# Half of an up-projection in Strassen units, merged rows added by DMA, embedding pairs moved

## The chip, the cores and the metric

The kernel runs on one NeuronCore of a Trainium2 chip. Its engines work side by side, each with a queue of its own: TensorE (PE, matmuls; its weight loads are shown as PEld), VectorE (DVE), ScalarE (ACT), GpSimd (POOL) and SyncE (SP, which here only issues DMAs). An engine takes its instructions in the order of its queue, and one that waits holds back all behind it. The metric is device time in microseconds; lower is better. Everything is float32 in DRAM; on PE each number is split into a high and a low part (type fp32r), and a product is three matmuls: high·high, high·low, low·high.

## The reference

One decoder layer, 512 tokens, width 2048 (all weights are inputs):

```python
proj = rmsnorm(x, attn_norm_g) @ w_in          # u, v_sgu, q, k, v_att, g_a, g_b
y_a = chunked_spatial_gating(gelu(u), rmsnorm(gelu(v_sgu)))     # 512 x 1024
y_b = stick_breaking_attention(rmsnorm(q), rmsnorm(k), v_att)   # 512 x 1024
merged = sigmoid(g_a) * (y_a @ w_up_a) + sigmoid(g_b) * (y_b @ w_up_b)
x = x + merged @ w_o
hid = rmsnorm(x, ffn_norm_g) @ w_ffn_in
x = x + (silu(gate) * up) @ w_ffn_out          # gate, up: halves of hid
x = x + sigmoid(rmsnorm(x, ple_norm_g) @ w_ple_gate) * (p @ w_ple)
```

## The kernel before

**Units.** Activations lie transposed (features by tokens) and are cut into blocks of 256 features by 512 tokens. One block against 256 columns of weights is a *unit*, and all units that sum to the same 256 outputs are a *pair* (`pair()`, class `Pair`). A unit is plain ("P": 12 matmuls of 512 columns) or Strassen ("S": seven products of a 2 x 2 scheme, 21 matmuls of 256 columns, or 7 of 512 and 7 of 256 where the pair asks for the `doubled` form with a bank of its own for each product). Tables such as `HALF` say until which pair of a stage each unit stays plain: the operand of a Strassen unit needs three more sums of the block, and plain pairs at a stage's start give time to make them.

**Operands.** A `Form` makes one operand: it loads the block (`fetch`), splits it into high and low (`plain_first`: ACT the high, DVE the low), later loads it a second time (`fetch_second`) and makes the sums. `tick()` is called once or twice per unit pair: it fetches one block, runs one step of one form or, if none is due, fetches one second half, and runs what `after(n, ...)` put n ticks ahead. `Weights` does the same for weights: two SP loads, a POOL DMA that adds in SBUF (L361), a split on ACT (L357) and DVE (L354), and two sums (L373). Four landing places and three split places are shared by all weights.

**Stages.** (1) w_in: q, k, v and gate pairs in four rounds, with attention of each round run beside the next pairs in steps of a tick (`attention`: stages a, m, b, c, d per block of 128 keys, then `finish`, which multiplies by v); then the gating half. Gate pairs are spilled to DRAM. (2) The up-projection: for each of 8 column blocks j a pair of w_up_b, then one of w_up_a, four plain units each. A gate block is loaded, scaled by the norm's row and put through the sigmoid; DVE multiplies it with the two banks (L1350), adds the b part to the a part (L1354), and SP stores the merged block (L1332, DRAM tensor mix). (3) w_o: eight pairs of eight units on mix, with x added (L792) and stored (DRAM tensor x). The last pairs of the embedding product p @ w_ple follow: two before the last addition, three after it. (4) w_ffn_in, 44 pairs; (5) w_ffn_out in three passes, added to x in DRAM by POOL's DMA (L1430); (6) the last gate.

**Order.** The order is written out by `tick` and `after`; within it a scheduler sets each engine's queue. The last pair of a matmul stage frees its operands unit by unit, and the next stage's take their places, so a stage's border is where operands come just in time.

## Time and profile before

| What | us |
|---|---|
| Median of 3 runs | 2669.71 |
| Lowest and highest | 2667.64, 2671.62 |
| Profiled execution | 2668.2 |
| Its span, first to last instruction | 2666.5 |
| PE busy in it | 2640.4 |
| Up-projection (first to last multiply by a gate) | 831.1 to 997.1 |

The profile records one execution. Busy time of a matmul includes its way through the array, so two matmuls in a row overlap in it; the price of one more matmul is the distance from start to start in the timeline. A row of waits names the instruction that waited and the one that ended the wait. In windows, each engine's busy time stands ahead of its instruction count, then come the granted clock of PE, the share of the DMA engines and GB/s.

### The profile page before, as it was taken

The numbers are of one execution on the slowest core, as the hardware profiler recorded it, in microseconds if no ns is written. First come the engines' busy times: TensorE is split into PE (matmuls) and PEld (weight loads), VectorE is DVE, ScalarE is ACT, GpSimd is POOL, SyncE is SP. The second block draws the span as 40 slices with busy tenths as digits, with TensorE's granted clock in tenths as the row PEclk, the third lists the DMA queues.
The fourth block names the chain that finished last, engine by engine and source line by source line (L and its number), as shares of the span: only waits on it lengthen the run. The fifth ranks groups of instructions, "written<-read, shape, count | busy, mean of one in ns | idle before, by whom it ended". The sixth has DMA issues, their size and how long they took to land.

```text
span 2666.5 us, 42598 instructions
## 1 busy us (share of the span) xinstructions
PE 2640.4 (99%) x15354; PEld 2312.4 (87%) x15354; DVE 2236.4 (84%) x3791; ACT 1413.9 (53%) x2245; POOL 453.4 (17%) x557
## 2 busy tenths in 40 slices
PE   8999999999999999999999999999999999999999
PEld 7888898888998888888888888888888888889898
DVE  8687878787887658989889888888889989989876
ACT  7656565655554334576444444444445445455643
POOL 0222322222220001101111111111110211211010
PEclk9999999999999999999999999999999999999999
DMA  7577777677775669988888878888787989988884
GB/s 227 158 190 174 185 173 187 171 182 197 179 188 186 214 212 264 239 265 223 220 218 207 210 194 207 203 203 202 197 209 223 263 220 277 226 248 246 252 229 134
DMA packets 293875, 560.16 MB, mean 210 GB/s; under 512 B 26400, under 2 KB 140832, under 8 KB 293664
## 3 DMA queue, kind: packets, MB, share of 16 engines
q1 hardware_dynamic: 231408, 442.08, 50.4%
q0 software_dynamic: 62256, 115.37, 27.0%
q8 instruction: 120, 1.97, 0.3%
q14 instruction: 91, 0.75, 0.1%
HBM read 505.97 MB, written 51.38 MB: 209 GB/s over the span
## 4 chain that ended last, share of the span: by engine, by line
PE 88%; DVE 5%; ACT 2%; DMA 2%; issue 1%; POOL 0%; SPq 0%; POOLq 0%; DVEq 0%; ACTq 0%
PE ps L683 49%; PE ps L295 10%; PE ps L296 10%; PE ps L294 10%; PE small L683 6%; DVE wlo L354 2%; DVE out L742 1%; PE small L1145 1%; PE small L1021 1%; DMA wholes<-x 1%; DMA wholes<-w_in 1%; ACT whi L357 1%; DVE wholes L373 0%; PE small L1095 0%; DVE parts L285 0%
## 5 line engine op out<-in xcount | busy, mean ns | idle before, releaser
L683 PE MATMUL ps<-parts,whi 128*128 128x512 f32 x4200 | 1404.7, 398 | 3.7 <-DVE out L787 3.1
L357 ACT ACTIVATE whi<-wholes 128x512 fp32r<-128x512 f32 (+3 forms) x941 | 872.5, 940 | 727.6 <-DVE wholes L373 270.5
L354 DVE TENSOR_TENSOR wlo<-wholes,whi 128x512 fp32r<-128x512 f32 (+3 forms) x941 | 982.7, 1079 | 65.8 <-ACT whi L357 64.0
L683 PEld LDWEIGHTS ps<-parts,wlo 128*128 128x128 f32 x4200 | 788.9, 188 | 178.4 <-DVE wlo L354 1.1
L683 PE MATMUL ps<-parts,wlo 128*128 128x256 f32 x4200 | 832.0, 279 | 0.0
L683 PEld LDWEIGHTS ps<-parts,whi 128*128 128x128 f32 x4200 | 676.4, 189 | 10.2 <-issue 4.5
L294 PE MATMUL ps<-parts,whi 128*128 128x256 f32 (+1 forms) x1822 | 598.9, 330 | 8.0 <-ACT parts L284 5.6
L295 PE MATMUL ps<-parts,whi 128*128 128x256 f32 (+1 forms) x1838 | 605.9, 330 | 0.8 <-DVE parts L285 0.8
L296 PE MATMUL ps<-parts,wlo 128*128 128x256 f32 (+1 forms) x1838 | 605.8, 330 | 0.0
L295 PEld LDWEIGHTS ps<-parts,whi 128*128 128x128 f32 x1838 | 348.4, 190 | 39.0 <-DVE parts L285 2.4
L294 PEld LDWEIGHTS ps<-parts,whi 128*128 128x128 f32 x1822 | 344.6, 190 | 41.5 <-ACT parts L284 6.7
L296 PEld LDWEIGHTS ps<-parts,wlo 128*128 128x128 f32 x1838 | 348.8, 190 | 30.8
L373 DVE TENSOR_TENSOR wholes<-wholes 128x256 f32<-128x256 f32 x822 | 345.1, 420 | 21.7 <-DMA wholes<-w_ffn_in 2.6
L742 DVE TENSOR_TENSOR out<-out,ps 128x256 f32<-128x256 f32 x490 | 202.9, 416 | 149.9 <-ACT out L739 149.4
L361 POOL DMA_DIRECT2D wholes<-w_ffn_in x170 | 148.0, 870 | 691.2 <-DVE wholes L373 197.4
L361 POOL DMA_DIRECT2D wholes<-w_in x132 | 116.3, 882 | 523.1 <-DMA wholes<-w_in 146.8
L683 PE MATMUL small<-parts,whi 128*128 128x512 f32 x480 | 190.3, 396 | 0.0
L285 DVE TENSOR_TENSOR parts<-wholes,parts 128x1024 fp32r<-128x1024 f32 (+3 forms) x148 | 138.1, 945 | 23.0 <-ACT parts L284 23.0
L284 ACT ACTIVATE parts<-wholes 128x1024 fp32r<-128x1024 f32 (+3 forms) x148 | 119.3, 830 | 55.1 <-DVE wholes L525 33.3
L739 ACT ACTIVATE out<-ps 128x256 f32<-128x256 f32 x258 | 95.7, 382 | 49.9 <-PE ps L683 46.4
L361 POOL DMA_DIRECT2D wholes<-w_ffn_out x64 | 55.6, 869 | 358.3 <-DMA wholes<-w_ffn_out 136.5
L1395 ACT ACTIVATE out<-out 128x512 f32<-128x512 f32 x44 | 27.9, 634 | 159.2 <-DVE out L1394 159.2
(123 smaller groups left out, 1750.2 us busy)
## 6 DMA issues: line engine op xcount, KB each, us to landing
wholes<-w_ffn_in SPq DMA_DIRECT2D x170, 384.0 KB, 5.6
wholes<-w_in SPq DMA_DIRECT2D x132, 384.0 KB, 5.0
wholes<-w_ffn_in SPq DMA_DIRECT2D x170, 256.0 KB, 4.8
wholes<-w_ffn_in POOLq DMA_DIRECT2D x170, 256.0 KB, 5.4
wholes<-w_in SPq DMA_DIRECT2D x132, 256.0 KB, 4.0
wholes<-w_in POOLq DMA_DIRECT2D x132, 256.0 KB, 5.0
wholes<-w_ffn_out SPq DMA_DIRECT2D x64, 384.0 KB, 6.3
wholes<-x SPq DMA_DIRECT2D x45, 512.0 KB, 5.6
```

The source lines that it names most:

```text
L284: return (nc.scalar.activation(hi, src, AF.Copy), nc.vector.tensor_tensor(out=lo, in0=src, in1=hi.bitcast(F32), op=ALU.subtract))
L285: nc.vector.tensor_tensor(out=lo, in0=src, in1=hi.bitcast(F32), op=ALU.subtract))
L294: nc.tensor.matmul(ps, sh, mh, start=start, stop=False)
L295: nc.tensor.matmul(ps, sh, ml, start=False, stop=False)
L296: return nc.tensor.matmul(ps, sl, mh, start=False, stop=stop)
L354: in_turn(nc.vector.tensor_tensor(out=self.lo[:, blocks], in0=r, in1=h.bitcast(F32), op=ALU.subtract))
L357: in_turn(nc.scalar.activation(h, r, AF.Copy))
L361: nc.gpsimd.dma_start(out=raw[:, 3:5], in_=self.src[:, 1:3], accum_op=ALU.add)
L373: in_turn(nc.vector.tensor_tensor(out=o, in0=x, in1=y, op=ALU.add))
L683: m = nc.tensor.matmul(out, l, r, start=first and k == 0, stop=last and k == 1)
L739: in_turn(nc.scalar.activation(out, x, AF.Copy, scale=scale))
L742: in_turn(nc.vector.tensor_tensor(out=out, in0=x, in1=y, op=op))
```

## The change

In words, by place:

- **Up-projection.** The order within j is now a, then b. The b operands become `late_form`, and `UP_UNTIL` makes w_up_b plain for units 0 and 1 in pair 0 and for units 2 and 3 in pairs 0 and 1: 26 of its 32 units are Strassen units, undoubled. y_a's first block takes its place at the other end of the arena.
- **Gates.** The scaling by the norm's row moves from the load to the spill, two ticks after the gate pair. In the up-projection each gate block is loaded one pair ahead.
- **Merge.** The a part goes to DRAM by SP; the b part is added to it there by a DMA of POOL.
- **Embedding pairs** 3 to 7 follow the b pairs 1 to 5 of the up-projection, with their operands loaded after pair 0.
- **Attention.** `finish(0)` runs one block later, ahead of `stage_b`, and the last block gets one tick more before `stage_d`; the first row of sums is kept in two small adds.
- **FFN.** `FFN_UNTIL` keeps units 2 and 3 plain in the second pair. The first pair's ending and the last gate's first ending run three ticks later.
- **tick()** does both a step of a form and a second fetch, where both are due. Gains are applied in the split itself (ACT with a scale, DVE with scalar_tensor_tensor).

```diff
+UP_UNTIL = 1, 1, 2, 2
+LATER = 3
+FFN_UNTIL = 1, 1, 2, 2, 2, 2, 2, 2
...
         if builds and builds[0].ready() and builds[0].arrived() and fits(builds[0].sizes):
             builds.popleft().step()
-        elif seconds and fits([(wholes, 5 * 256, "old")]):
+        if seconds:
             f = (urgent or seconds)[0]
-            if f.used or not any(b.stage == f.stage and b.ready() and not b.there
-                                 for b in list(builds)[:AHEAD]):
+            if (f.used or not any(b.stage == f.stage and b.ready() and not b.there
+                                  for b in builds)) and fits([(wholes, 5 * 256, "old")]):
                 f.fetch_second()
...
+            if i == NT + 1:
+                finish(0)
             stage_b(j)
             yield 1
-            if i == NT:
-                finish(0)
             stage_c(j)
             if ahead:
                 stage_m(*ahead[0])
             yield 1
+            if not ahead:
+                yield 1
             stage_d(h, j)
...
-            for b in "ba":
-                plan((w_up_a if b == "a" else w_up_b)[j], "PPPP")
+            for b in "ab":
+                plan((w_up_a if b == "a" else w_up_b)[j],
+                     "PPPP" if b == "a" else now("SSSS", UP_UNTIL, j))
+            if 0 < j < 6:
+                planned.append((w_ple[j + 2].rearrange("p (b c) -> p b c", b=4), 1, "P"))
...
+    rows = deque([load(gate_spill["a", 0], 1024, "low")])
+    halves = [(j, b) for j in range(KU) for b in "ab"]
+    for (j, b), later in zip(halves, halves[1:] + [None]):
+        s = rows.popleft()
+        g = s.f()
+        after(1, lambda g=g: nc.scalar.activation(g, g, AF.Sigmoid))
+        if later:
+            after(1, lambda later=later: rows.append(
+                load(gate_spill[later[1], later[0]], 1024, "low")))
+        pr = pair([ys[b, i] for i in range(4)], last=j == KU - 1, j=j,
+                  until=UP_UNTIL if b == "b" else None)
+        if pr.n["S"]:
+            tt(g, g, pr.out(), ALU.mult)
+        else:
             for h, ps in zip((g[:, :T], g[:, T:]), pr.ends()):
-                nc.vector.tensor_tensor(out=h, in0=h, in1=ps, op=ALU.mult)
+                tt(h, h, ps, ALU.mult)
+        def store_merged(b=b, j=j, s=s):
+            if b == "a":
+                nc.sync.dma_start(out=spill["mix", j], in_=s.f())
             else:
-                nc.vector.tensor_tensor(out=g, in0=g, in1=part[j].f(), op=ALU.add)
-                after(1, lambda j=j, s=s: store("mix", j, s))
+                nc.gpsimd.dma_start(out=spill["mix", j], in_=s.f(), accum_op=ALU.add)
+                after(1, lambda: there.add(("mix", j)))
+            give(s)
+        after(1, store_merged)
+        if b == "b":
+            if not j:
+                ple_operands()
+            elif j < 6:
+                ple_pair(j + 2)
+                if j == 5:
+                    ple_done()
...
-        return plain_form((lambda: y_a[i]) if c == "a" else lambda: load(y_spill[i]),
-                          lambda: len(y_done) == 8, raw=0 if c == "a" else 1024,
-                          far=c == "b")
+        if c == "a":
+            return plain_form(lambda: y_a[i], ready, raw=0, how="low" if i else ("high", "low"))
+        return late_form(lambda size=1024: load(y_spill[i], size), ready, far=True)
...
-            nc.sync.dma_start(out=d, in_=o)
-            gate_spill[w, i] = d
+            d = gate_spill[w, i] = tc.dram_tile([P, 1024], F32, name=nm("gsp"))
+            def spill_gate(o=o, d=d):
+                scaled(o, row1)
+                nc.sync.dma_start(out=d, in_=o)
+            after(2, spill_gate)
...
-        if j == KU - 1:
-            ple_pair(3)
-            ple_pair(4)
-        h = raw.popleft()
         pr.onto(h.f())
...
-    for j in range(5, 8):
-        ple_pair(j)
-    ple_done()
...
-        o = pair(fs, last=m == KH - 1, j=m, until=HALF, doubled=7).out()
-        if m == 0:
-            row2 = norm2.row()
+        o = pair(fs, last=m == KH - 1, j=m, until=FFN_UNTIL, doubled=7).out()
         st = Staged(hidden(m, o))
-        st.step()
+        if m:
+            st.step()
+        else:
+            after(LATER, st.step)
...
+            if j:
+                close(o)
+            else:
+                rest()
+                after(LATER, lambda close=close, o=o: close(o))
```

**ACT, attention of the first round.** L1138 (now L1151) is the exponential of a block of 128 keys, L1147 (now L1160) the copy that ends `finish(0)`, L739 and L751 belong to the pair that runs beside. Before, the copy stands three rows behind the fourth exponential, whose result `finish(0)` multiplies on PE:

```order
L357 ACTIVATE whi_80<-wholes 128x1280
L1138 ACTIVATE wholes<-wholes 128x512
L739 ACTIVATE out_1467<-ps_1291 128x256
L739 ACTIVATE out_1467<-ps_1296 128x256
L1147 ACTIVATE wholes<-small_1449 128x512
L739 ACTIVATE out_1467<-ps_1301 128x256
```

Now, around the same copy:

```order
L1133 ACTIVATE parts<-wholes 128x128
L751 ACTIVATE out_1465<-ps_1292 128x256
L751 ACTIVATE out_1465<-ps_1297 128x256
L751 ACTIVATE out_1465<-ps_1302 128x256
L360 ACTIVATE whi_80<-wholes 128x512
L751 ACTIVATE p_197_1470<-ps_1313 128x256
L1108 ACTIVATE wholes<-small_1505,rr_719 128x384
L360 ACTIVATE whi_78<-wholes 128x1280
L1110 ACTIVATE wholes<-wholes 128x384
L1111 ACTIVATE wholes<-wholes 128x384
L1109 ACTIVATE wholes<-small_1505,rr_719 128x384
L1151 ACTIVATE wholes<-wholes 128x128
```

The fourth exponential stands just ahead of the first of these rows and the copy two rows behind the last: the next block's steps, its exponential among them, now come in between.

**SP, end of the up-projection.** mix_8246 (before) and mix_8290 (now) are the last of the eight merged blocks; a row with mix on the left stores, one with mix on the right loads. Before:

```order
L1332 DMA mix_8246<-wholes 128x1024
L337 DMA wholes<-w_o 128x1024
L516 DMA wholes<-mix_8246 128x1024
L337 DMA wholes<-w_o 128x1024
L516 DMA wholes<-mix_8242 128x1024
L516 DMA wholes<-xT 128x1024
```

Now (the store is of the a part alone):

```order
L1382 DMA mix_8290<-wholes 128x1024
L342 DMA wholes<-w_o 128x2x256
L344 DMA wholes<-w_o 128x768
L519 DMA wholes<-xT 128x1024
L342 DMA wholes<-w_o 128x2x256
L344 DMA wholes<-w_o 128x768
L340 DMA wholes<-w_o 128x1024
L519 DMA wholes<-mix_8289 128x1024
L340 DMA wholes<-w_o 128x1024
L519 DMA wholes<-mix_8284 128x1024
L519 DMA wholes<-mix_8290 128x1024
L519 DMA wholes<-mix_8285 128x1024
```

Seven weight and x loads of w_o's first pairs and the first load of the seventh block have come between the store and the load, and the first of the second loads (mix_8284, mix_8285) stand right beside it.

**POOL, same place.** Before, POOL goes from w_in's weight adds straight to w_o's (L361, the weight add):

```order
L361 DMA wholes<-w_in 128x512
L919 TENSOR_TENSOR rr_7678<-ms_7671,expo 128x4
L361 DMA wholes<-w_in 128x512 x6
L361 DMA wholes<-w_o 128x512 x26
L966 TENSOR_TENSOR cols_10884<-mean_10882,expo 128x4
```

Now (L364, the weight add; L1384, the add into mix):

```order
L1384 DMA mix_8289<-wholes 128x1024
L364 DMA wholes<-w_o 128x512 x2
L1384 DMA mix_8290<-wholes 128x1024
L364 DMA wholes<-w_o 128x512 x24
L364 DMA wholes<-w_ffn_in 128x512
```

The add of the last merged block stands behind two of w_o's weight adds and ahead of the other 24.

More of the change, by code (lines that the diff above doesn't have):

```diff
@@ L604, in plain_form @@
     def plain_form(src, ready=always, gain=None, raw=1024, how="low", far=False):
+        hows = [how] * 2 if isinstance(how, str) else how
         def steps(form):
-            hi, lo = form.blocks = parts.take(1024, how), parts.take(1024, how)
+            hi, lo = form.blocks = [parts.take(1024, h) for h in hows]
             w = form.raw()
```

94 lines of the change are left out of this document (45 added, 49 removed).

## The prediction

> **What bounds the kernel now.** The page comes first: its span, its engines and the chain that ended last.
>
> ```profile
> span 2666.5 us, 42598 instructions
> PE 2640.4 (99%) x15354; PEld 2312.4 (87%) x15354; DVE 2236.4 (84%) x3791; ACT 1413.9 (53%) x2245; POOL 453.4 (17%) x557
> PE 88%; DVE 5%; ACT 2%; DMA 2%; issue 1%; POOL 0%; SPq 0%; POOLq 0%; DVEq 0%; ACTq 0%
> ```
>
> TensorE (PE) is busy for all but 2666.5 − 2640.4 = 26.1 us. So time comes from two sources only: fewer nanoseconds of matmuls, or fewer of those 26 us. Next, the view of who waited for whom, for PE (waiter, releaser, total us, times, longest):
>
> ```profile
> PE ps L683 <- DVE out L787: 3.1, 1, 3.1
> PE small L1145 <- ACT wholes L1138: 2.5, 3, 0.8
> PE small L1133 <- DVE parts L1126: 1.6, 4, 0.7
> PE small L932 <- DVE diag L930: 1.0, 1, 1.0
> PE small L1145 <- issue: 0.8, 1, 0.8
> PE ps L294 <- ACT out L873: 0.6, 1, 0.6
> ```
>
> These six are 9.6 us, and the change touches the place of each. The longest costs more than it shows. Windows (us, busy PE, PEld, DVE, ACT, POOL, then granted clock, DMA share, GB/s) around it:
>
> ```profile
> 1044.00:1047.00 3.00, 0.28 (x2) 0.00 (x0) 3.00 (x4) 0.91 (x3) 0.89 (x1) 1.00 0.93 352
> 1049.00:1052.00 3.00, 3.00 (x12) 2.60 (x11) 2.69 (x5) 2.70 (x3) 0.88 (x1) 0.50 1.03 292
> ```
>
> PE stands still for 3.1 us while DVE is busy without a gap, and some 2 us after it resumes the clock is 0.50: 12 matmuls in 3 us. If that holds for about 3.4 us, which I take from how long the slow rows last, it costs 1.7 us more: 4.8 us in all. The Trainium skill (TensorE: Matmul & The Clock Gate, "What's actually happening") has the clock halved after an idle window of about 3.4 us, free-running. By that rule 3.1 us of idling need not halve it, and the stop would be worth 3.1 (the sum below 1.2 us smaller, as an estimate); here the clock halved, so the row decides.
>
> **Up-projection of attention's half.** A plain unit (one 256-row block of weights) is 12 matmuls of 512 columns, a Strassen unit 21 of 256, since this call does not ask for the doubled form. The timeline of PE has the price of each, first and last of a steady run (start, us, line):
>
> ```profile
> 940.03 0.39 PE L295 MATMUL ps<-parts,whi 128*128 128x512 f32 x1
> ...
> 957.03 0.39 PE L295 MATMUL ps<-parts,whi 128*128 128x512 f32 x1
> 1025.79 0.28 PE L296 MATMUL ps<-parts,wlo 128*128 128x256 f32 x1
> ...
> 1027.95 0.28 PE L296 MATMUL ps<-parts,wlo 128*128 128x256 f32 x1
> ```
>
> The first two are 75 matmuls apart: 0.2267 us each. The last two are 18 apart: 0.120 us each. So 12 × 0.2267 = 2.72 us against 21 × 0.120 = 2.52: 0.20 us less per unit. The table turns 26 of the 32 units of w_up_b into Strassen units, −5.2 us, and FFN_UNTIL turns two units of the FFN's second pair the other way, +0.4. **PE work: −4.8 us.** The Trainium skill (same page, "Back-to-back issue gap") gives N / 2.4 + 2.5 ns, which is 215.8 and 109.2 ns: 0.30 us a unit and −7.1 us as an estimate. With it the sum below would be −13.3. The rows are slower, at 256 above all, and I keep them.
>
> The new units cost other engines work: per two units a wider weight split, two sums and a DMA add, then the mix of four banks. The cover is this stage of the window view (and the stage before it, where the 16 gate scalings of 1.22 us go):
>
> ```profile
> 100.00:830.00 730.00, 722.21 (x4601) 643.97 (x4600) 593.51 (x1044) 441.33 (x919) 182.14 (x245) 1.00 0.71 182
> 830.00:996.00 166.00, 165.26 (x728) 136.20 (x727) 100.13 (x108) 59.09 (x59) 0.88 (x1) 1.00 0.61 204
> L354 DVE TENSOR_TENSOR wlo<-wholes,whi 128x1280 fp32r<-128x1280 f32 x405 | 603.4, 1490 | 29.7 <-ACT whi L357 29.4
> L373 DVE TENSOR_TENSOR wholes<-wholes 128x256 f32<-128x256 f32 x810 | 341.6, 422 | 21.6 <-DMA wholes<-w_ffn_in 2.6 <-DVE wlo L354 1.9 <-DMA wholes<-w_ffn_out 1.6
> L1212 DVE TENSOR_TENSOR wholes<-wholes 128x1024 f32<-128x1024 f32 x20 | 24.4, 1222 | 26.1 <-DMA wholes<-gsp 26.1
> ```
>
> DVE takes 1.22 us for 1024 columns, 0.69 for 512 (a row of L1350 further down) and 0.42 for 256. Thirteen weights grow by 1.8 us each (1.49 + 0.69 + 2 × 0.42 − 1.22), seven mixes add 2.8 (five adds of 0.42, one of 0.69), and 16 scalings and 8 merges of 1.22 leave: some +14 us on 100 of 166. DVE stays idle for over 50 us, so I cost it at nothing. Without that cover each weight would hold PE for up to its 1.8 us, 23 us in all. The scalings add 20 us to a stage where DVE has 136 us free: nothing.
>
> **Attention's ticks.** finish(0) now comes after the next block's last step, and the last block's running sums get a tick more. A tick is half a weight pair, about 2.4 us, against waits of at most 0.8: all of L1145 (2.5 + 0.8) and L1133 (1.6) should go. **−4.9**, bounds −3.3 and −4.9, if one of them merely becomes another wait.
>
> **Stage borders.** Into the up-projection, PE waits for the split of y (starts of 831.50, 832.10, 833.36 and 833.70):
>
> ```profile
> 831.50 0.39 PE L296 MATMUL ps<-parts,wlo 128*128 128x512 f32 x1
> 832.10 0.73 PE L294 MATMUL ps<-parts,whi 128*128 128x512 f32 x2 [0.21 <-ACT parts L284]
> 833.36 0.50 PE L295 MATMUL ps<-parts,whi 128*128 128x512 f32 x1 [0.52 <-DVE parts L285]
> 833.70 0.39 PE L296 MATMUL ps<-parts,wlo 128*128 128x512 f32 x1
> ```
>
> Four starts take 2.20 us instead of 0.91. Now y_a comes first, is resident, and its first block has a place before the old operands go: **−1.3** (0 to −1.3). The copies of the embedding pairs (L873) no longer end back to back: **−0.6**. Norm 3 is read three ticks later, which takes some of the 1.0 at L932: **−0.5** (0 to −1.0).
>
> **The stop at 1044.** It is DVE's queue: the bank that PE wants is freed by L787, behind second-half work of the w_o operands. The new tick() builds and fetches a second half in one tick, so those loads stand further ahead: 68 matmuls of 512 and 32 of 256 (19.3 us) between the last one and the freeing add, before 59 and 23 (16.1). That is 3.1 us more for the same DVE work, about the stop. With its slow clock it is worth −4.8; DVE's list there is no shorter, so I take **−3.4** (0 to −4.8).
>
> **The merged rows.** Here the change adds a wait. Before, the last merged block goes by one DVE add, a store and a load through SP; now a multiply, a POOL DMA that adds in DRAM, and the load. Landing times (median us) and the old chain's SP rows:
>
> ```profile
> x<-out POOLq DMA_DIRECT2D x16, 512.0 KB, 8.9
> wholes<-mix SPq DMA_DIRECT2D x16, 512.0 KB, 5.5
> wholes<-w_o SPq DMA_DIRECT2D x26, 384.0 KB, 5.6
> wholes<-w_o POOLq DMA_DIRECT2D x26, 256.0 KB, 5.7
> L284 ACT ACTIVATE parts<-wholes 128x1024 fp32r<-128x1024 f32 x72 | 74.5, 1051 | 30.4 <-DVE wholes L525 10.7 <-DMA wholes<-y 10.0 <-DMA wholes<-mix 8.3
> 996.44 0.69 DVE L1350 TENSOR_TENSOR wholes<-wholes,ps 128x512 f32<-128x512 f32 x1 [0.67 <-PE ps L296]
> 998.41 0.33 SPq L1332 DMA_DIRECT2D mix<-wholes  x1
> 1001.83 0.33 SPq L516 DMA_DIRECT2D wholes<-mix  x1
> ```
>
> Call PE's entry into w_o t0 (996.3 there). The last unit of the first w_o pair wants this block at t0 + 7 × 2.72 = 19.0. New chain: the mix's last add, two splits and the multiply on DVE (0.69 + 3 × 1.22), t0 + 4.4; on POOL it stands behind a weight add that waits for a w_o load (5.6 us), t0 + 5.7; landing 8.9, t0 + 14.6; load 5.5, t0 + 20.1; split on ACT and DVE (1.05 + 1.22), t0 + 22.4, and the first matmuls need both halves. That is **3.3 us late**. A landing as quick as the plain store (3.4 us from row to row) and the multiply alone would be on time: 0. The POOL add and the load at about 1 us over their medians, with the slow clock, give +6.7. I take +3.3 and, as it sits near what slowed the clock at 1047, +0.7: **+4.0**. Behind the waiting load on SP stand w_o's next weights; four landing places hold them off.
>
> **The FFN's start** loses 5 × 2.72 us of embedding pairs that used to cover the last x1 block. Its store and load issue:
>
> ```profile
> 1170.66 0.33 SPq L1376 DMA_DIRECT2D x<-wholes  x1
> 1178.22 0.38 SPq L516 DMA_DIRECT2D wholes<-x  x1
> x<-wholes SPq DMA_DIRECT2D x16, 512.0 KB, 4.9
> wholes<-x SPq DMA_DIRECT2D x45, 512.0 KB, 5.6
> ```
>
> From w_o's end: what stands on DVE up to the add (7 × 0.42 of the mix, 0.69, a split of 1.22, two half splits of 0.69, the add's 1.22) 7.5 us, store 4.9, load 5.6, split of halves about 2 = 20.0, wanted at 19.0 plus some 0.5 us of norm matmuls: **+0.5** (0 to +6, if the load is slow enough to slow the clock too). Were the pairs still there it would be nothing.
>
> **Sum:** −4.8 − 4.9 − 1.3 − 0.6 − 0.5 − 3.4 + 4.0 + 0.5 = −11.0 us. The profiled execution took 2668.2 us (span 2666.5 and 1.7 around it), so 2657.2; the median of the runs is 1.5 above it: **2658.7 us**.
>
> **Rivals.** *The waits move* (19%): the merged chain and the x1 chain both come at their slow ends with half clock (+6.7, +6), and the stop at 1044 stays (0). Then −12.1 + 12.7 = +0.6 against the profiled time, about 2670. For it: they sit where the windows around 1044 show the DMA engines busy for 0.93 and 1.03 of the time. Against: each chain alone has to miss by 5 us.
>
> *POOL's queue holds the weights* (9%, slower): POOL runs in order, and a mix add waiting for its multiply or its earlier store stands before weight adds. If it holds them for longer than the four landing places cover, about two weights of 4.9 us, PE waits in each of the eight pairs, 3.3 us a time: 26 us, less the 15.5 of the certain gains and the stop, about 2680. For it: 8.9 us per add, 5.7 per weight add. Against: POOL is busy for 0.88 of 166 us in that stage today, and the store ends a whole pair (10 us) earlier.
>
> *The short matmul is no gain* (inside the forecast's lower chance, 4%): if the weight load, not the columns, sets 0.120 us and grows beside the up stage's other reads, at 0.130 a Strassen unit equals a plain one; −4.8 becomes 0 and the time 2663.5. The w_o rows above, with the same form, speak against it.
>
> **How the numbers follow.** A measurement of this kernel can tell about 0.2%, 5.3 us, from no change: 2664.4 and 2675.1 are the bounds. Forecast 68%, the third rival 4%: both faster, 72%. First rival 19%: same. Second 9%: slower. The range runs from every gain in full without a late merged block (−17, with the 2 us that the sum may be off, 2650) to just under the first rival, 2669.
>
> **What would show it.** Right: PE's waits have no L1145 and L1133 rows (under their new lines), 256-column rows start 0.120 us apart in the up stage, and one wait of about 3 us stands some 19 us into w_o, released by ACT's or DVE's split of mix. Wrong: more than 5 us lost at w_o or the FFN's start, waits in every up pair, or the stop before w_o's third pair unshortened with clock 0.50 behind it.

## The result, and the profile after

| | Before | Changed |
|---|---|---|
| Median of 10 runs each, us | 2669.33 | 2674.82 |
| Lowest and highest, us | 2665.47, 2674.16 | 2673.19, 2680.28 |
| Profiled execution, us | 2668.2 | 2673.2 |

The ratio is 1.0019, 95% interval [1.001, 1.0027]: 5 us slower, where the prediction had 2658.7 us, range 2650 to 2669. First the page of the changed kernel, its span, its PE row and its chain by engine:

```profile
span 2671.5 us, 43268 instructions
PE 2639.6 (99%) x15571; PEld 2318.6 (87%) x15571; DVE 2269.1 (85%) x3907; ACT 1422.2 (53%) x2266; POOL 457.5 (17%) x577
PE 84%; DMA 7%; DVE 5%; ACT 2%; issue 2%; SPq 0%; POOL 0%; POOLq 0%; ACTq 0%; DVEq 0%
```

PE's idle time went from 26.1 to 31.9 us, and transfers have come into the chain: 7%, before 2%. To place the loss, both executions are cut at three matmuls of PE that they share: the start of the up-projection (1.4 us early, with the twelve matmuls of 256 columns that end w_in), the start of w_o and the first doubled matmul of w_o. In the two middle stretches, *lost* is what is left when each matmul of 512 columns counts 0.2267 us and each of 256 columns 0.1200.

| Stretch | Before | Changed | Difference | Predicted |
|---|---|---|---|---|
| To the up-projection | 819.2 | 813.4 | −5.8 | −4.9 |
| Up-projection and w_o's start, as matmuls, without the embedding pairs | 218.3 | 213.1 | −5.2 | −5.2 |
| Lost in the up-projection | 1.5 | 9.0 | +7.5 | −1.3 |
| Lost at w_o's start | 0.0 | 12.7 | +12.7 | +4.0 |
| From there on, without the embedding pairs | 1627.5 − 13.6 | 1609.7 | −4.2 | −3.6 |

(13.6 us are the five embedding pairs, 60 matmuls of 0.2267; the last prediction is −3.4 + 0.5 − 0.6 − 0.5 + 0.4.) The differences add up to +5.0, as the two executions do. Three rows came near the forecast, 1.5 us better together. Two are off by 8.8 and 8.7 us, and they make the miss of 16 us. PE's waits from 845 to 1045 us (waiter, releaser, total us, times, longest) make 14.1 us of the 21.7 lost there; most of the rest is matmuls at half clock behind two of the stops:

```profile
PE ps L297 <- ACT parts L287: 7.0, 1, 7.0
PE ps L299 <- DVE wlo L357: 2.8, 3, 1.3
PE ps L298 <- DVE parts L288: 2.3, 3, 1.6
PE ps L297 <- ACT out L718: 2.0, 1, 2.0
```

None of them comes from a lack of DVE time: DVE got idler, 60.6 us busy of 120 where it had 68.6, while the DMA engines' share rose. The windows from 870 to 990 us, of before and then of the changed kernel with two stretches behind stops (us, busy PE, PEld, DVE, ACT, POOL, clock, DMA share, GB/s):

```profile
870.00:990.00 120.00, 120.00 (x531) 99.38 (x530) 68.59 (x74) 40.12 (x39) 0.00 (x0) 1.00 0.64 215
```

```profile
870.00:990.00 120.00, 116.43 (x696) 103.43 (x695) 60.59 (x89) 45.83 (x58) 10.82 (x13) 0.97 0.83 231
935.60:940.80 5.20, 5.20 (x12) 4.12 (x13) 3.28 (x6) 0.27 (x1) 0.87 (x1) 0.50 0.94 247
1034.00:1041.00 7.00, 5.59 (x15) 4.16 (x16) 6.07 (x8) 3.87 (x5) 0.89 (x1) 0.56 0.94 327
```

What the engines wait for is transfers. In the view of waits, SP's queue from 828 to 1000 us of before (up to 1050 it is 15.9 us in 8), and then of the changed kernel from 828 to 1050:

```profile
SPq L516 <- DMA mix<-wholes: 14.0, 7, 2.2
```

```profile
SPq L519 <- DMA mix<-wholes: 112.2, 15, 10.2
```

SP stands for 112 us, half of the stretch, behind the stores of a parts and the DMA adds of b parts. The chain of waits shows how (start, us, what):

```profile
892.74 8.15 DMA mix<-wholes
...
900.91 0.33 SPq L519
...
902.81 8.45 DMA mix<-wholes
...
911.28 0.33 SPq L519
...
912.20 6.28 DMA wholes<-w_up_b
...
919.86 7.77 DMA mix<-wholes
```

The SP row behind each of them (L519) is the load of a gate row into the place of the block that is still being sent. Behind it on SP stand the next w_up_b weights. The row then comes late to ACT, where its sigmoid (L1368) is in front of the copies of the pair's banks (L718), which PE waits for, and in front of a weight split (L360). ACT's timeline (start, us, instruction, idle before it):

```profile
918.13 2.44 ACT L360 ACTIVATE whi<-wholes 128x1280 fp32r<-128x1280 f32 x3
931.46 1.06 ACT L1368 ACTIVATE wholes<-wholes 128x1024 f32<-128x1024 f32 x1 [10.89 <-DMA wholes<-gsp]
932.42 1.04 ACT L360 ACTIVATE whi<-wholes 128x1024 fp32r<-128x1024 f32 x1
933.37 1.06 ACT L718 ACTIVATE out<-ps 128x512 f32<-128x512 f32 x2
```

PE stopped at 932.0 for 2.0 us, then for 0.7, and its clock was 0.50 from 935.6 to 940.8. At w_o's start the chain is the one predicted, with other times:

```profile
1011.87 6.30 DMA wholes<-w_o
...
1019.47 9.33 DMA mix<-wholes
...
1029.19 4.63 DMA wholes<-mix
...
1033.84 1.06 ACT parts L287
```

### The profile page after: what moved, and what is told of

Read it like the earlier page. It is cut to its first block, busy times and chain, and to the rows that moved or that the text cites. A ratio compares the mean times of both kernels' runs of the same rounds, so it can differ in the third digit from the quotient of the medians.

```text
span 2671.5 us, 43268 instructions
## 1 busy us (share of the span) xinstructions
PE 2639.6 (99%) x15571; PEld 2318.6 (87%) x15571; DVE 2269.1 (85%) x3907; ACT 1422.2 (53%) x2266; POOL 457.5 (17%) x577
## 4 chain that ended last, share of the span: by engine, by line
PE 84%; DMA 7%; DVE 5%; ACT 2%; issue 2%; SPq 0%; POOL 0%; POOLq 0%; ACTq 0%; DVEq 0%
PE ps L695 52%; PE ps L299 8%; PE ps L298 8%; PE ps L297 8%; PE small L695 6%; DMA mix<-wholes 3%; DMA wholes<-w_up_b 2%; DVE wlo L357 1%; DVE parts L288 1%; DVE wholes L528 1%; DVE out L754 1%; PE small L1158 1%; PE small L1032 1%; PE small L1106 1%; DMA wholes<-w_ffn_out 0%
## 5 line engine op out<-in xcount | busy, mean ns | idle before, releaser
L360 ACT ACTIVATE whi<-wholes 128x512 fp32r<-128x512 f32 (+2 forms) x953 | 882.4, 940 | 736.9 <-DVE wholes L376 300.9
L357 DVE TENSOR_TENSOR wlo<-wholes,whi 128x512 fp32r<-128x512 f32 (+2 forms) x953 | 990.4, 1074 | 35.3 <-ACT whi L360 34.7
L695 PEld LDWEIGHTS ps<-parts,wlo 128*128 128x128 f32 x4200 | 788.2, 188 | 180.2 <-DVE wlo L357 2.4
L695 PEld LDWEIGHTS ps<-parts,whi 128*128 128x128 f32 x4200 | 676.5, 189 | 8.5 <-issue 1.8
L297 PE MATMUL ps<-parts,whi 128*128 128x256 f32 (+1 forms) x1893 | 609.6, 323 | 15.4 <-ACT parts L287 11.9
L299 PE MATMUL ps<-parts,wlo 128*128 128x256 f32 (+1 forms) x1910 | 617.8, 324 | 3.2 <-DVE wlo L357 3.2
L298 PE MATMUL ps<-parts,whi 128*128 128x256 f32 (+1 forms) x1910 | 617.7, 324 | 2.3 <-DVE parts L288 2.3
L297 PEld LDWEIGHTS ps<-parts,whi 128*128 128x128 f32 x1893 | 359.7, 191 | 45.2 <-ACT parts L287 12.7
L298 PEld LDWEIGHTS ps<-parts,whi 128*128 128x128 f32 x1910 | 363.3, 190 | 37.9 <-DVE parts L288 5.1
L299 PEld LDWEIGHTS ps<-parts,wlo 128*128 128x128 f32 x1910 | 363.6, 190 | 33.1 <-DVE wlo L357 5.7
L376 DVE TENSOR_TENSOR wholes<-wholes 128x256 f32<-128x256 f32 (+1 forms) x846 | 355.5, 420 | 30.1 <-DMA wholes<-w_up_b 11.2
L364 POOL DMA_DIRECT2D wholes<-w_ffn_in x169 | 147.1, 871 | 704.9 <-DVE wholes L376 204.5
L364 POOL DMA_DIRECT2D wholes<-w_in x132 | 116.8, 886 | 546.5 <-DVE wholes L376 132.1
L288 DVE TENSOR_TENSOR parts<-wholes,parts 128x1024 fp32r<-128x1024 f32 (+3 forms) x143 | 127.4, 904 | 16.1 <-ACT parts L287 16.1
L287 ACT ACTIVATE parts<-wholes 128x1024 fp32r<-128x1024 f32 (+3 forms) x143 | 110.9, 798 | 55.0 <-DVE wholes L528 37.3
L751 ACT ACTIVATE out<-ps 128x256 f32<-128x256 f32 x258 | 96.0, 385 | 49.6 <-PE ps L695 46.1
L364 POOL DMA_DIRECT2D wholes<-w_ffn_out x64 | 55.6, 870 | 357.0 <-DMA wholes<-w_ffn_out 117.5
```

Of the source, the lines that this page charges most:

```text
L287: return (nc.scalar.activation(hi, src, AF.Copy), nc.vector.tensor_tensor(out=lo, in0=src, in1=hi.bitcast(F32), op=ALU.subtract))
L288: nc.vector.tensor_tensor(out=lo, in0=src, in1=hi.bitcast(F32), op=ALU.subtract))
L297: nc.tensor.matmul(ps, sh, mh, start=start, stop=False)
L298: nc.tensor.matmul(ps, sh, ml, start=False, stop=False)
L299: return nc.tensor.matmul(ps, sl, mh, start=False, stop=stop)
L357: in_turn(nc.vector.tensor_tensor(out=self.lo[:, blocks], in0=r, in1=h.bitcast(F32), op=ALU.subtract))
```

## The experiments

A diff is against the changed kernel unless another is named; ratios are to the kernel before, measured on the same chip. The runs come from several chips, on which the kernel before took 2669.3 to 2671.1 us, so rows of the table are compared by their ratios. The two columns of lost time are from one profiled execution each, worked out as above.

| Run | Median us | Ratio, 95% interval | Lost in up | Lost at w_o |
|---|---|---|---|---|
| (changed kernel) | 2674.82 | 1.0019 [1.001, 1.0027] | 9.0 | 12.7 |
| gate_early | 2671.38 | 1.0000 [0.9992, 1.0009] | 8.9 | 9.0 |
| gate_early_last | 2671.56 | 1.0000 [0.9991, 1.0008] | 5.5 | 3.3 |
| rows_oldest | 2676.43 | 1.0022 [1.0013, 1.0032] | 9.8 | 10.3 |
| merge_by_dve | 2660.33 | 0.9956 [0.9944, 0.9968] | 0.1 | 5.4 |
| merge_by_dve_oldest | 2661.35 | 0.9967 [0.9955, 0.998] | 0.1 | 2.0 |
| plain_units | 2663.69 | 0.9973 [0.9962, 0.9983] | 0.0 | 6.5 |
| merge_by_dve_plain | 2658.23 | 0.9957 [0.9945, 0.997] | 0.0 | 0.0 |
| add_as_store | 2661.61 | 0.9967 [0.9955, 0.998] | 0.1 | 7.6 |
| pairs_back | 2663.41 | 0.9977 [0.9968, 0.9986] | 0.1 | 8.5 |
| rows_behind_weights | 2685.89 | 1.0063 [1.005, 1.0075] | 18.1 | 11.9 |
| sigmoid_late | 2671.97 | 1.0007 [0.9997, 1.0017] | 10.0 | 10.2 |
| rows_behind_sigmoid_late | 2668.45 | 0.9991 [0.9981, 1.0001] | 5.5 | 9.3 |
| merge_by_dve_sigmoid_late | 2659.55 | 0.9952 [0.9936, 0.9968] | 0.1 | 6.0 |
| merge_by_dve_oldest_late | 2660.87 | 0.9966 [0.9954, 0.9978] | 0.1 | 1.3 |
| merge_by_dve_pairs_back | 2662.35 | 0.9966 [0.9954, 0.9979] | 3.3 | 9.2 |
| merge_by_dve_plain_pairs_back | 2659.74 | 0.996 [0.9946, 0.9974] | 0.0 | 0.0 |
| ticks_only | 2666.92 | 0.9987 [0.9978, 0.9996] | 1.1 | 0.0 |
| rest_of_change | 2672.56 | 1.0015 [1.0003, 1.0026] | 1.2 | 4.0 |

The profiled executions of gate_early and gate_early_last (2666.9 and 2663.2 us) lie 4.5 and 8.4 us under their medians, so their lost time is too small for what is typical; nothing below rests on it. Those of the other runs lie within 4 us of their medians.

### Undoing one part at a time

**gate_early**, the row loaded at the head of the pair, ahead of the store:

```diff
-            after(1, lambda later=later: rows.append(
-                load(gate_spill[later[1], later[0]], 1024, "low")))
+            rows.append(load(gate_spill[later[1], later[0]], 1024, "low"))
```

> Theory (place reuse): in the changed kernel the next gate row is loaded into the place of the block whose store or DMA add was issued just before, so SP stands until that transfer has landed (106.9 us in 13 waits behind mix), and the weights queued behind it on SP come late. Loading the row at the head of the pair, into another place, ahead of the store, leaves everything else as it is. Then the 13 waits fall below 30 us in all, the stops at 931, 962, 995 and 1014 us (10.8 us with their slow clock) go, and the last merged block comes some 5 us earlier: 2674.8 - 11 to - 17, about 2660. Rival 1 (the DMA add is slow by itself, about 8.7 us a landing, and the time goes at w_o's start): no more than 3 us gained, 2672 or above. Rival 2 (the Strassen units' wider weights and sums are what comes late): the stops stay, 2672 or above.

SP's waits behind mix stayed (107.2 us in 14), and 3 to 5 us were won. The scheduler had set the load on SP right behind the next older transfer that frees a place, so the test did not take the wait away; neither theory was decided.

**merge_by_dve**, the merge alone undone:

```diff
-        def store_merged(b=b, j=j, s=s):
-            if b == "a":
-                nc.sync.dma_start(out=spill["mix", j], in_=s.f())
-            else:
-                nc.gpsimd.dma_start(out=spill["mix", j], in_=s.f(), accum_op=ALU.add)
-                after(1, lambda: there.add(("mix", j)))
-            give(s)
-        after(1, store_merged)
+        if b == "a":
+            part = s
+        else:
+            tt(g, g, part.f(), ALU.add)
+            give(part)
+            after(1, lambda j=j, s=s: store("mix", j, s))
```

> The merge alone is undone: the a part stays in SBUF, DVE adds it, one store by SP for each column block, no add by POOL; the Strassen units, the order and the row loads stay. Place reuse: half of the transfers that SP waits for are gone and the last block's chain is short again (a store of about 5 us and a load of 5.5): SP's waits behind mix fall to 20 to 50 us and the time to about 2658 to 2664. Rival 2 (Strassen units' weights are late): the stops of the up-projection stay, only the 7 us stop at w_o's start shrinks, about 2668.

Inside the expected range; in the profile no stop is left before w_o. SP's waits behind mix are 18.9 us in 8. Of the 16.2 us less lost, 6.2 come back behind the first doubled matmul of w_o (1615.9 us there, 1609.7 in the changed kernel): PE's waits there are 7.4 us in all, and 2.5 in the changed kernel.

**plain_units**, the units alone undone:

```diff
-                     "PPPP" if b == "a" else now("SSSS", UP_UNTIL, j))
+                     "PPPP")
...
-                  until=UP_UNTIL if b == "b" else None)
+                  until=None)
...
-        return late_form(lambda size=1024: load(y_spill[i], size), ready, far=True)
+        return plain_form(lambda: load(y_spill[i]), ready, far=True)
```

> The Strassen units of w_up_b alone are undone (all 32 plain, y loaded once); the merge by DMA and the row loads stay. Place reuse: SP still waits for about 100 us behind mix in 12 or 13 waits, PE's work grows by 5.2 us, the stops stay in part: 2673 to 2682. Rival 2 (the units' weights are the cause): the stops go and the time is 2674.8 + 5.2 - 11 to - 20, 2660 to 2668.

This came out as the rival had it: though SP still stood 53 us behind mix, no stop was left in the up-projection, and the kernel got faster with 5.2 us more matmuls. So there is no single culprit; the merge and the units each take the slack that the other needs.

**gate_early_last**, gate_early with the eighth block merged by DVE as in merge_by_dve:

```diff
+        if j == KU - 1:
+            if b == "a":
+                part = s
+                continue
+            tt(g, g, part.f(), ALU.add)
+            give(part)
...
+            elif j == KU - 1:
+                store("mix", j, s)
+                return
```

> Row loads at the head of the pair as in gate_early, and the last column block alone is merged by DVE with one store. Place reuse plus a long last chain: the stop of 7 us at w_o's start with its slow clock (13 us in all) falls to 3 us or less, and the time to about 2655 to 2658, under gate_early by 3 to 6 us. If gate_early alone has already removed that stop, the two are equal within 2 us.

Its median equals gate_early's. In the one profiled execution w_o's start lost 3.3 us instead of 9.0, but that execution is 8.4 us under the median: left open.

### The place, and the add itself

**rows_oldest**, the same tick, another place (without `"low"`, `load` takes the place given back longest ago):

```diff
-                load(gate_spill[later[1], later[0]], 1024, "low")))
+                load(gate_spill[later[1], later[0]])))
```

> The gate rows are loaded at the same tick as in the changed kernel, but each into the place that has been free longest (four places in turn, some three pairs or 30 us after the store that read it) instead of the one freed at that tick. gate_early gave only one pair of distance (SP's waits stayed at 107 us), so it did not settle the theory. Place reuse: SP's waits behind mix fall from 112 us below 30 us, the stops at 931, 962, 995 and 1014 us go, and the time is 2660 to 2665. Rival 3 (traffic: the DMA engines are busy for 0.83 of 870 to 990 us, before 0.64, and every landing there is longer): SP's waits shrink, but the landings of w_up_b stay at 7 to 8 us, the stops stay, and the time is 2669 to 2675.

It missed: 102.4 us behind mix in 15 waits, and as slow as the changed kernel by the ratio. From the fourth block on the load stands on SP right behind the store that frees its place, although four places take turns: it looks as if the scheduler brings a load forward until the place lets it go no further. ACT then waited for no row, but for weights:

```profile
ACT whi L360 <- DMA wholes<-w_up_b: 47.3, 6, 11.8
```

**add_as_store**, a plain store by POOL instead of the add; the sum then lacks the a part:

```diff
-                nc.gpsimd.dma_start(out=spill["mix", j], in_=s.f(), accum_op=ALU.add)
+                nc.gpsimd.dma_start(out=spill["mix", j], in_=s.f())
```

> POOL stores the b part over the a part instead of adding it (the a part is left out of the sum); places, queues and order stay. If reading and adding in DRAM is what makes the transfer long, its landing falls from 8.7 us to 5.5 or less, the stop at w_o's start from 7 us to under 4, and the time to 2664 to 2668. If the landing is long because of what is queued on the DMA engines beside it, as for the a part's plain store (8.5 us), it stays at 7 us or more and the time at 2671 to 2675.

13 us faster, more than expected, though the landing fell less than expected (to 6.5, not 5.5 us). On SP, POOL, ACT and DVE the instructions of the stage come in the same order as in the changed kernel, so the add is all that differs. Landing of the transfers into mix (KB each, median us from issue), first of the changed kernel, then of add_as_store:

```profile
mix<-wholes SPq DMA_DIRECT2D x8, 512.0 KB, 8.5
mix<-wholes POOLq DMA_DIRECT2D x8, 512.0 KB, 8.7
```

```profile
mix<-wholes SPq DMA_DIRECT2D x8, 512.0 KB, 8.6
mix<-wholes POOLq DMA_DIRECT2D x8, 512.0 KB, 6.5
```

In this stage the add took 2.2 us longer than a plain store of the same bytes at the same place in the same queue, and it did so before anything had stopped: the four adds ahead of the stop at 932 landed in 5.2, 9.2, 8.2 and 7.8 us, the four stores in 3.1, 8.1, 4.9 and 6.4. It is no fixed price of adding, however. In two other runs, plain_units and pairs_back (below), the adds are still there and land as quickly as the stores here:

```profile
mix<-wholes POOLq DMA_DIRECT2D x8, 512.0 KB, 6.4
mix<-wholes POOLq DMA_DIRECT2D x8, 512.0 KB, 6.5
```

So what the add costs depends on what else the stage moves. The a part's store stays at 8.6, so that one is long for another reason, and the DMA share stays too (0.82). SP still stands 93.5 us behind mix. What changed is how long ACT waits for rows, first in the changed kernel, then in add_as_store (845 to 1010 us):

```profile
ACT wholes L1368 <- DMA wholes<-gsp: 50.7, 9, 10.9
```

```profile
ACT wholes L1368 <- DMA wholes<-gsp: 27.9, 9, 6.7
```

Its waits for w_up_b fell as well, from 20.6 to 10.2 us, and that was enough: 9.0 us lost in the up-projection became 0.1, and at w_o's start 12.7 became 7.6. There the last store landed in 8.8 us, hardly less than the add's 9.3; the gain is that POOL issued it 8.1 us behind w_o's start and not 13.2.

**merge_by_dve_oldest**, merge_by_dve with rows_oldest's place:

> merge_by_dve (2660.3 us) with the gate rows loaded into the place free longest. Place reuse: its last 19 us of SP's waits behind mix go; as PE waits nowhere in its up-projection, the time stays at 2658 to 2661. If it is faster by over 2 us, SP's waits there delayed w_o's first weights.

Equal, as expected. **ticks_only** is the kernel before with the part of the change from `a_tiles` to `attention` (finish(0) one block later, the extra tick, the two small adds):

> The kernel before with the change of attention's ticks alone (finish one block later, one tick more before the last stage_d, the first row of sums in two adds). The prediction's term: PE's waits for the exponential's copy and for the parts go, -4.9 us (-3.3 to -4.9): ratio 0.9982, 2664.5 to 2666 where the kernel before has 2669.3. Rival (one wait becomes another): within 1 us of the kernel before.

The waits for the copy and for the parts are gone, the up-projection starts 4.2 us earlier, and the ratio says −3.5 us (interval −5.9 to −1.1): the term holds, by the median at its lower end. In the profiled execution the stop before w_o's third pair is longer (4.8 us of excess instead of 3.3).

### Two theories of why late transfers stop PE

**pairs_back**: the embedding pairs 3 to 7 go from the up-projection back to the last pair of w_o and behind it, as in the kernel before.

```diff
-            elif j < 6:
-                ple_pair(j + 2)
...
+        if j == KU - 1:
+            ple_pair(3)
+            ple_pair(4)
...
+    for j in range(5, 8):
+        ple_pair(j)
+    ple_done()
```

> The embedding pairs 3 to 7 go back to the end of w_o; the rest is the changed kernel's. New theory (a ring of transfers): in the changed kernel each column block of the up-projection goes once round a ring: the a part's store (8.5 us), the gate row that waits on SP for that store's place, the w_up_b weights behind it on SP (6.3), POOL's weight add and behind it the add into mix (7.8), and the next gate row that waits for that. The adds into mix are issued 27.1, 26.4, 24.1, 24.6 and 24.4 us apart, whereas PE's work for a block is 23.7 us with an embedding pair and 21.0 without. So without the pairs the ring still takes 23.5 to 24.5 us a block and PE stands longer: its stops between 860 us and w_o come to 15 to 25 us and the time to 2674 to 2682. Rival 3 (traffic: the pairs' loads and stores in the stage): 2664 to 2669.

The ring fell. The adds into mix on POOL follow PE's work for a block, 21.0 us. The first and the last of five in a row:

```profile
882.91 0.89 POOL L1384 DMA_DIRECT2D mix<-wholes  x1 [5.08 <-DVE wholes L376]
...
967.93 0.89 POOL L1384 DMA_DIRECT2D mix<-wholes  x1 [3.53 <-DVE wholes L376]
```

85.02 us for four blocks is 21.3 a block (the next add, at the stage's end, follows 24.4 us later). No ring of transfers sets a pace above that; the time fell by 11 us although the DMA share rose to 0.89. Rival 3 named about the right time for the wrong reason, since the stage became denser. The adds land in 6.5 us here, as shown above, and the a parts' stores in 10.5.

**rows_behind_weights**: each row's load held behind the weight loads then known, three ticks into the pair (`i` in the first line is the last SP load of `Weights`):

```diff
+            chain["load"] = i.ins.name
...
+    def behind(src):
+        row = take(1024)
+        i = nc.sync.dma_start(out=row.f(), in_=src).ins
+        tc.add_manual_dep(i, chain["load"], mybir.DependencyInfo(
+            mybir.DependencyClass.NoSync, mybir.DependencyReason.DATA),
+            reason="behind the weights")
+        rows.append(row)
...
-            after(1, lambda later=later: rows.append(
-                load(gate_spill[later[1], later[0]], 1024, "low")))
+            after(3, lambda later=later: behind(gate_spill[later[1], later[0]]))
```

> rows_oldest did not free SP, because the scheduler sets each row's load on SP just behind the transfer whose place it takes, wherever that is. Here each row's load is held back to stand behind the weight loads known three ticks into the pair: the load that waits for the add into mix now stands behind the two loads of the next w_up_b weights, not ahead of them. Ring: the weights leave the ring on that side, the adds into mix come 23 to 25 us apart, most stops of the up-projection go, and the time is 2662 to 2669. If SP's order is not a link of the ring, the stops stay and the time is 2672 or above.

The slowest of all, where the ring had the time fall. ACT waits no more for w_up_b, but longer for rows, and PE with it:

```profile
ACT wholes L1379 <- DMA wholes<-gsp: 55.9, 7, 13.0
```

**merge_by_dve_plain**, the edits of merge_by_dve and plain_units together:

> merge_by_dve with all units of w_up_b plain: against merge_by_dve (2660.3 us) it measures what the Strassen units are worth where nothing waits. The prediction's term: 26 units of 0.20 us, so 5.2 us longer, 2665 to 2666. Rival (a 256-column matmul is no gain in this stage): within 1.5 us of 2660.

Missed: by the ratios (0.9957 and 0.9956) equal to merge_by_dve, not 5 us slower. That is the rival's time, but not its reason. The stretch from the up-projection to the first doubled matmul takes 231.9 us here and 232.2 there: the 5.2 us of matmuls that the units save (0.1200 us apart in the up-projection) are lost again, 5.4 us, at w_o's start.

**rest_of_change**: the kernel before with attention's ticks, the new tick(), gains in the split and the later endings. In it the pairs of the FFN go by FFN_UNTIL and their weights by HALF, so two units of its second pair multiply weights split for the other form.

> The kernel before with the rest of the change alone (attention's ticks, the new tick(), gains in the split, the later endings), without the up-projection's units, merge by DMA, early rows, moved embedding pairs and FFN_UNTIL. By the prediction's terms: ticks -3.5 (measured by ticks_only), the stop at 1044 -3.4 (0 to -4.8), norm 3 -0.5: 2669.7 - 7.4, about 2662 (2660 to 2666). If the stop at 1044 went only because the stage ahead of it changed, 2666.

Above the expected range: the stop before w_o's third pair is there, and another 4.0 us are lost at w_o's start.

```profile
PE ps L695 <- DVE out L799: 5.9, 2, 4.7
```

**sigmoid_late**:

```diff
-        after(1, lambda g=g: nc.scalar.activation(g, g, AF.Sigmoid))
+        after(3, lambda g=g: nc.scalar.activation(g, g, AF.Sigmoid))
```

> The changed kernel with each gate row's sigmoid put three ticks into its pair instead of one; loads, merge and units stay. The ring fell: in pairs_back the adds into mix follow PE at 21 us. Theory 4 (the row at the head of ACT): the row that came late through SP stops ACT at its sigmoid (50.7 us in 9 waits of up to 10.9 us from 845 to 1010 us), and behind the sigmoid on ACT stand the two bank copies and the weight splits that PE needs; rows_behind_weights, which brings the weights early and the rows later, has 55.9 us of it (longest 13.0) and is the slowest. With the sigmoid behind the copies, ACT's waits for rows fall under 25 us, the stops at 931 and 962 us go, and of the 21.7 us lost between the first matmul of the up-projection and the first doubled one of w_o 10 to 14 stay (w_o's start, weights): 2663 to 2668. Rival (weights held on SP are the stops): lost time 19 us or more, 2672 or above.

Half of it came: ACT's waits for rows fell from 50.7 to 14.0 us and the stops at 932 and 962 went. But others came at 942, 945, 971 and 972, where ACT and DVE split weights, and the 20.2 us lost in all are what the rival had said:

```profile
ACT whi L360 <- DMA wholes<-w_up_b: 36.7, 7, 8.2
ACT wholes L1368 <- DMA wholes<-gsp: 14.0, 5, 5.8
```

**rows_behind_sigmoid_late**, the edits of rows_behind_weights and sigmoid_late together:

> rows_behind_weights (2685.9 us) with the sigmoid three ticks into the pair: weights pass the waiting row on SP, and the copies pass it on ACT. Theory 4 with both late arrivals out of the way: the 30 us lost in that stretch fall to 8 to 12 (w_o's start is left), 2661 to 2668. If delaying the row was bad for another reason (DVE's multiply, the banks it frees), it stays above 2675.

Half a microsecond above the range: some 19 us faster by the ratio than rows_behind_weights by changing the sigmoid's place alone, and with 5.5 us lost in the up-projection better than either. So both late arrivals count, the row at the head of ACT and the weights behind the row on SP; whichever is spared, the other stops PE. That some of it stays would fit add_as_store, where shorter transfers took it away, but no run joins the two.

### Versions with the merge undone

**merge_by_dve_sigmoid_late**, **merge_by_dve_oldest_late** and **merge_by_dve_pairs_back** put edits shown above (the sigmoid's, the place's, the pairs') on merge_by_dve:

> merge_by_dve (2660.3 us) with the sigmoid three ticks into the pair. There ACT waits 14 us for rows but PE has no stop before w_o: no more than 2 us gained, 2658 to 2661; a slower result would say that the multiply now comes late for the banks.

> merge_by_dve_oldest (2661.4 us; 2.2 us lost in the stretch) with the sigmoid three ticks in: equal within 2 us, 2659 to 2663. It is the candidate with the Strassen units; merge_by_dve_plain (2658.2 us) has 5.2 us more matmuls in that stretch and loses nothing there, so what decides between them lies behind it.

> merge_by_dve (2660.3 us) with the embedding pairs back at the end of w_o, Strassen units kept. What is left there: 5.6 us lost before the first doubled matmul of w_o, 1.9 us at the first FFN pair (x1's split), which the pairs would cover again, and a fuller up-projection without them. Theory: 2655 to 2659. If the fuller stage stops PE (DVE has no pairs to catch up in), 2661 or above.

The first two are equal to their parents. The third is no faster than merge_by_dve: in its profile the up-projection loses 3.3 us and w_o's start 9.2, more than with the pairs (0.1 and 5.4). So the same five pairs that hurt beside the DMA merge do not hurt beside the DVE merge. That they give cover there, because DVE has more to do, is a reading that no run tests.

**merge_by_dve_plain_pairs_back** puts the pairs' edit on merge_by_dve_plain:

> merge_by_dve_plain (2658.2 us) with the embedding pairs back at the end of w_o: nothing of the up-projection's change is left but the order a, b, the gates scaled at the spill and the row loaded a pair ahead. Its stop at the first FFN pair (1.9 us with slow clock) goes; the stop before w_o's third pair may come back, as in ticks_only (4.8 us) and rest_of_change (4.8 us): 2655 to 2662. If it comes back, moving the pairs is what had removed it; if not, the up-projection's lighter DVE is.

Equal to merge_by_dve_plain within its runs. The stop before w_o's third pair did not come back, so it goes without the moved pairs too.

Best are the versions without the DMA merge: merge_by_dve_sigmoid_late, merge_by_dve and merge_by_dve_plain, 0.43% to 0.48% under the kernel before and 0.6% to 0.7% under the changed one, with intervals that overlap.

## Why the prediction was wrong, step by step

**Matmuls of the units: right.** 0.1200 us apart in the up-projection, 5.2 us less; the third rival is out.

**Attention's ticks: right**, −4.2 to the up-projection in the trace of ticks_only and −5.8 with the rest of the change, where −4.9 was forecast.

**"I cost it at nothing": the step that failed.** The prediction weighed the wider splits, sums, mixes and the later rows against DVE's free time alone. DVE did get idler; what the stage lacked was time for the transfers. The a store and the DMA add put two of 8.5 and 8.7 us into each block, each with a gate row waiting on SP for the place that it frees, and the weights behind that row. The cost was 9.0 us lost instead of a gain of 1.3. It goes with the add alone (0.1 in add_as_store), with the whole merge (0.1), with the units (0.0) and with the moved pairs (0.1): beside the merge by DMA the stage carries any two of add, units and pairs, but not the three. The a part's store was not taken out by itself. How the embedding pairs add to it (an SP store that waits for ACT's copy, 13.0 us in 5 waits, and a landing place for half the usual work, are candidates in the trace) was not tried by itself.

**The last merged block: right chain, one time wrong.** With w_o's start at t0 = 1006.3 the landing took 9.3 us (predicted 8.9), the load with SP's issue 5.0 (5.5), and the split followed. But POOL issued the add at t0 + 13.2, not t0 + 5.7: the weight add in front of it waited for a w_o load that SP issued only at 1011.87. The chain to that load starts with the add of the block before, which landed at 1003.0: only then could SP load the last gate row, which came at 1006.8, and behind its sigmoid on ACT stood the split that freed the load's landing place. That is +7.5 on a term of +3.3, and the longer stop slowed the clock as well: 12.7 us against +4.0. "Four landing places hold them off" is the sentence that fell.

**The rival on POOL's queue** had the right kind of hold, weights behind a transfer into mix, and the wrong queue: it was SP's. The argument against it, that the a part's store ends a whole pair earlier, looked at the wrong transfer: the row waits for the place of each, not for mix.

**The stop before w_o's third pair: right that it goes, with a reason that is not enough.** It is gone in the changed kernel, and the part of the execution that holds it came to −4.2 us where −3.6 was forecast. But rest_of_change has the new tick() and still stops for 4.7 us; merge_by_dve_plain_pairs_back has neither the units nor the moved pairs and does not stop. What is left between the two is the order a, b, the scaling at the spill, the early gate row, the places of y's and attention's tiles, FFN_UNTIL and the x rows, which rest_of_change loads one pair ahead, as the kernel before does, and the changed kernel in their own pair (the list of the change does not name this); they were not told apart. So the new tick() alone does not remove the stop, and that the forecast came near here is in part luck.

**The first rival** gave a nearer time (about 2670), but only the first of its three terms came, and larger than it had it: behind the first doubled matmul of w_o no wait of PE in the changed kernel is over 0.8 us, so neither the x1 chain nor the stop at 1044 took part.

**What the prediction named as proof of error came:** more than 5 us lost at w_o's start. The stops of the up-projection stood in three of eight blocks, not in every one.

## What to carry to other kernels

When a store or an add in DRAM is put into a steady stage, write down which later load takes the SBUF place that it frees and what stands behind that load on its queue: a load cannot be early if its place is not free, whatever tick it is written at. Cover has to be counted for each queue, SP's first, and not only for the engine that does the arithmetic. Where several additions share one slack, undoing each alone will look like the cure, and so the smallest one (here a plain store instead of the add) tells most.

## What the runs showed of the hardware

In the changed kernel a 512 KB transfer from SBUF to DRAM that adds took a median of 8.7 us to land, and in add_as_store a plain store in the same place of the same queue 6.5. But such adds took 6.4 and 6.5 us in plain_units and pairs_back, so a median from one stage is no price for another. The Trainium skill (DMA: Bandwidth & Descriptors, "Rules for kernel authors") says that an accumulating transfer reads its destination and writes it later; the 8.7 us would fit that, the 6.4 and 6.5 do not ask for it, and no run separates the reading from the adding.

A stop of 2.0 us and one of 0.7, two matmuls apart, were followed by 5.2 us at clock 0.50 (935.6 to 940.8). The stop of 7.0 us at w_o's start was followed by rows 0.43 us apart up to 1040.2. Single stops of 1.3 and 1.6 us (at 995 and 1015) were followed by no slow rows. The Trainium skill (TensorE: Matmul & The Clock Gate, "What's actually happening") has the clock halved after at least one idle window of about 3.4 us; the stop of 7.0 us agrees, and the pair of 2.0 and 0.7, shorter than that even together, does not.
